# The embedding's products join the end of the recurrence's fill stream and wait in DRAM; ScalarE writes a pair's first right-hand side

## The chip, the cores and the metric

The kernel runs on one core of one Trainium2 chip. The metric is the device time of one launch in microseconds (us); the median of three runs is compared. The engines are named as in the profile: PE is TensorE (PEld its weight loads), DVE is VectorE, ACT is ScalarE, POOL is GpSimd, SP is SyncE, which here only issues transfers. ACTq and SPq are the sequencers of ACT and SP at work on the issue of a DMA.

## The reference, cut to what matters

One decoder layer over 512 tokens of width 2048, all in fp32:

```
z = rms_norm(x) @ w_in                  # r, k, v, lora inputs, gates, pool input
y_rwkv = delta-rule recurrence over r, w, k, v, kk, a (16 heads of 64), group norm, bonus, gate
y_pool = causal window means, a small linear map per group, gate
x = x + concat(y_rwkv, y_pool) @ w_out
gate = sigmoid(x @ w_pg + b_pg)
x = x + gate * (p @ w_ple)              # p: 512 x 256, w_ple: 256 x 2048
out = rms_norm(x)
```

The embedding term p @ w_ple depends on nothing that the kernel computes: both factors are inputs.

## The kernel before, in words

Every large product is made of three fp32r products (high by high, high by low, low by high) of operands that are split into a rounded part and a rest: `split` and `wsplit` cast on ACT and subtract on DVE. One such product of 128 by 128 weights with 512 columns is called a product below.

**Recurrence.** The 16 heads are worked through as 8 pairs j, each in 8 chunks ch of 64 tokens (`recur`). A chunk is a chain of small steps: py on PE (`py <- sbd, ar`), the right-hand side zs on DVE (`zs <- py, mv`, L721), pu on PE, two copies to uv on ACT (L731), ps on PE, the new state sbd on DVE (L742; L740 in the first chunk), and again py. In the first chunk there is no py: zs is a plain copy of mv on DVE (L725), where mv is what ACT copied out of the accumulator pmv (L648) in `gather`, before `recur` starts. While such a step runs on DVE or ACT, PE works on a stream of unrelated products (`stream`): the projections z of later pairs and the 16 units of the pool group (`pool_unit`, tile names zb and pp). `pump(n)` takes about n products from the stream, in units of 3, and carries what it overdrew to the next call. HC is the fill of the three legs of a chunk (py to pu, pu to ps, ps to py), H1 to H5 and HX are that of places in `gather` and between the pairs. All of PE's instructions of this part keep the order in which they are written. DVE and ACT take the work in an order that the scheduler fixes when the program is compiled.

**Between the parts.** After the last pair the stream is pumped by H2, `finish` turns the last pair's output on PE (pyt), scales it (yo) and writes it to the DRAM tensor yd (`yd <- yo`). The pools of the recurrence are then closed (`rw`, about a hundred kilobytes of each partition, among them) and the rest of the stream is drained. Then p is turned on PE (ppt) and split into phi and plo. At the start of the kernel the pool `xp` is closed in the same way ahead of `rw`; its last use is the turning of the parameters on PE (pt_prm, L296). The pool units of the stream use no tile of `rw`. The pool `ymp`, which takes the memory that `rw` left, gets the 16 rows of yd back (yin, three buffers) and their split halves yhi and ylo.

**Projections.** w_out and then w_pg are streamed in 4 column blocks ec of 512 (`proj`, accumulators acc_o and acc_g, 16 steps k by 4 token tiles tt by 3 products each). After a block of w_out the new x is added on DVE, written to x2d, and turned on PE (px) for the second projection. `embed(ec)` makes one block of p @ w_ple: 24 products, 4 copies to SBUF on ACT (L923). `embed(0)` stands behind the last block of w_out, `embed(ec + 1)` behind block ec of w_pg, ahead of that block's `gate`. In this part PE's order is the scheduler's. Accumulators rotate over five banks.

Of the kernel before, what the change touches and what calls it, by code (L numbers as in the profile page):

```python
# [34 lines left out]
def trunk_kernel(ctx: ExitStack, tc: tile.TileContext, x, p, norm_g, w_in, mu, w0, w_up, a0, a_up,  # L35
# [123 lines left out]
    def tr(*a):  # L159
        i = nc.tensor.transpose(*a)  # L160
        return tc.keep_in_program_order(i) if pin[0] else i

    def mm3(ps, wh, wl, xh, xl, first, last):
        mm(ps, wh, xh, start=first, stop=False)
        mm(ps, wh, xl, start=False, stop=False)
        mm(ps, wl, xh, start=False, stop=last)


    plan, ready = [], {}
# [23 lines left out]
    for j in range(NJ):  # L193
        if j + 1 < NJ:
            jobs += [("z", nm, j + 1) for nm in "krv"]
        jobs += [("b", None, n_ + i) for i in range(nfill[j])]
        n_ += nfill[j]
        if j + 1 < NJ:
            jobs += [("z", "g", j + 1)]
    plan_cols(O_L, "l")  # L200
    for kind, nm, j in jobs:
        if kind == "z":
            plan_cols({"r": O_R, "k": O_K, "v": O_V, "g": O_G}[nm] + j * P, f"{nm}{j}")
        else:
            g, i = j // 4, j % 2
            if j % 4 < 2:
                plan_cols(O_U + g * 256 + i * P, f"b{j}")
            else:
                plan_cols(O_GP + g * 256 + i * P, f"b{j}")
                plan.append((f"wp{j}", 0, w_pool[0, g, :, i * P:(i + 1) * P].rearrange("(k p) n -> p k n", p=P), 2, P))  # L210
# [174 lines left out]
    def pool_unit(n):  # L385
# [31 lines left out]
        nc.vector.scalar_tensor_tensor(sgp, pq, dp(73, m), sgp, ALU.mult, ALU.mult)  # L417
        nc.scalar.dma_start(out=yd[NJ + m], in_=sgp)

    def stream():  # L420
        for kind, nm, j in jobs:
            if kind == "b":
                yield from pool_unit(j)
                continue
            ps = psA.tile([P, T], F32, name=f"z{nm}{j}", tag="acc")
            yield from zcols(ps, f"{nm}{j}")
            t_ = rw.tile([P, T], F32, name=f"s{nm}{j}", tag=f"s{nm}", bufs=2)
            if nm == "g":
                silu2(ps, t_)
            else:  # L430
                shifted(ps, t_, {"r": 0, "k": 8, "v": 16}[nm] + j)
            zt[nm, j] = t_
# [18 lines left out]

    pws, kks, late = {}, {}, [None]

    H1, H2, H3, H4, H5 = 6, 16, 20, 6, 10

    def decay_and_rate(j):

# [156 lines left out]
    def gather(j):  # L614
# [26 lines left out]
        for u in range(8):  # L641
            for par in range(2):
# [2 lines left out]
                mm(ps[pb:pb + 64, u, :], mt[kb:kb + 64, par, u, 1 - par, :],  # L645
                   uv[kb:kb + 64, 2 * (u // 2) + par, 64 * h:64 * h + 64], start=True, stop=True)
        mv = rw.tile([P, 4, P], F32, name=f"mv{j}", tag="mv")
        nc.scalar.copy(mv.rearrange("p q (h t) -> p (q h) t", h=2), ps)  # L648

        d.update(uv=uv, bkn=bkn, mv=mv)  # L650
# [40 lines left out]
    def recur(j, work, between):  # L691
# [17 lines left out]
        for ch in range(NCH):  # L709
# [8 lines left out]
            if ch > 0:  # L718
                mm(py[:, sl], ar[:, q, 2 * par:2 * par + 2, :], cur, start=ch in (1, 4), stop=True,
                                 skip_group_check=True)  # L720
                lead[0] = nc.vector.tensor_tensor(zs[pb:pb + 64], py[pb:pb + 64, sl], mv[pb:pb + 64, q, :], ALU.add)  # L721
                step()
                pump(HC1)
            else:
                nc.vector.tensor_copy(zs[pb:pb + 64], mv[pb:pb + 64, q, :])  # L725

            psu = psS.tile([P, T], F32, name=f"pu{j}_{ch}", tag="s")
            mm(psu[:, 0:P], x1[:, 2 * q:2 * q + 2, :], zs, start=True, stop=True)
# [71 lines left out]

        pending.append(finish)

    HC, HT, HX = (7, 7, 8), 130, 24
    HS, HN = 9, 3
    pending = []
    need("k", 0)
# [13 lines left out]
    for j in range(NJ):  # L820
        def between():
            pump(H3)
            if j + 1 < NJ:
                scores(j + 1)
                pump(H2)

        if j + 1 < NJ:
            prepare(j + 1)
        recur(j, invert(j + 1) if j + 1 < NJ else iter(()), between)
        if j + 1 < NJ:  # L830
            gather(j + 1)
    pump(H2)
    pending.pop()()
    s2a.close()
    psB = ctx.enter_context(tc.tile_pool(name="psB", bufs=3, space=PSUM))
    lp = ctx.enter_context(tc.tile_pool(name="lp", bufs=1))
    pn = []
    for h in range(2):
        t_ = lp.tile([P, 2, DPLE], F32, name=f"pn{h}", tag="ple", bufs=4)
        nc.scalar.dma_start(out=t_, in_=p[256 * h:256 * h + 256, :].rearrange("(t p) q -> p t q", p=P))  # L840
        pn.append(t_)
    phi = lp.tile([P, 2, T], F32R, name="phi", bufs=1)
    plo = lp.tile([P, 2, T], F32R, name="plo", bufs=1)
    pump(10 ** 6)
    pin[0] = False
    for k in range(2):
        pt = psM.tile([P, T], F32, name=f"ppt{k}", tag="m")
        for tt in range(NT):
            nc.tensor.transpose(pt[:, tt * P:(tt + 1) * P], pn[tt // 2][:, tt % 2, k * P:(k + 1) * P], ident)
        split(phi[:, k, :], plo[:, k, :], pt)  # L850
    sy = ctx.enter_context(ExitStack())
    ymp = sy.enter_context(tc.tile_pool(name="ymp", bufs=1))
    yhi = ymp.tile([P, KT, T], F32R, name="yhi")
# [11 lines left out]
    EC = 512  # L865
    KEEP = 8
    TP = 40
    AS = (3,)
# [8 lines left out]
    def proj(w, hi_, lo_, ec, nm, ks=range(KT), tts=range(NT), keep=None):  # L877
        acc = {tt: acc_tile(f"acc_{nm}{ec}_{tt}") for tt in tts}
        if keep is not None:
            acc = {tt: [acc[tt]] if tt < NT - 1 else [acc[tt][:, 0:EC // 2], acc_tile("acc_h")[:, 0:EC // 2]]  # L880
                   for tt in tts}
        for i, k in enumerate(ks):
            src = w[k * P:(k + 1) * P, ec * EC:(ec + 1) * EC].unsqueeze(1)
            if keep is None or i < KT - KEEP:
                wh, wl = wsplit(src, 1, EC, f"{nm}{ec}_{k}")
            else:
                raw = wp.tile([P, 1, EC], F32, name=f"raw_{nm}{ec}_{k}", tag="raw")
                nc.sync.dma_start(out=raw, in_=src)
                own = i < KT - 4
                wh = (kp_ if own else wp).tile([P, 1, EC], F32R, name=f"whk{k}", tag=f"whk{k}" if own else "whi")  # L890
                wl = (kp_ if own else wp).tile([P, 1, EC], F32R, name=f"wlk{k}", tag=f"wlk{k}" if own else "wlo")
                split(wh, wl, raw)
                keep[k] = (wh, wl)
                continue
            for tt in tts:
                ts_ = slice(tt * P, (tt + 1) * P)
                parts = acc[tt] if keep is not None else [acc[tt]]
                hw = EC // len(parts)
                for h, a_ in enumerate(parts):
                    hc = slice(h * hw, h * hw + hw)  # L900
                    mm3(a_, hi_[:, k, ts_], lo_[:, k, ts_], wh[:, 0, hc], wl[:, 0, hc], i == 0, i == KT - 1)
        return acc

    ples = {}

    def embed(ec, pool):
        es = slice(ec * EC, (ec + 1) * EC)
        src = w_ple[:, es].rearrange("(k p) n -> p k n", p=P)
        ph, pl = [], []
        for k in range(2):  # L910
            a_, b_ = wsplit(src[:, k:k + 1, :], 1, EC, f"ple{ec}_{k}")
            ph.append(a_)
            pl.append(b_)
        ple = []
        for tt in range(NT):
            ts_ = slice(tt * P, (tt + 1) * P)
            pq = psM.tile([P, EC], F32, name=f"pple{ec}_{tt}", tag="m")
            for k in range(2):
                nc.tensor.matmul(pq, phi[:, k, ts_], ph[k][:, 0, :], start=k == 0, stop=False)  # L919
                nc.tensor.matmul(pq, phi[:, k, ts_], pl[k][:, 0, :], start=False, stop=False)  # L920
                nc.tensor.matmul(pq, plo[:, k, ts_], ph[k][:, 0, :], start=False, stop=k == 1)  # L921
            t_ = pool.tile([P, EC], F32, name=f"ple{ec}_{tt}", tag="ple", bufs=4)
            nc.scalar.copy(t_, pq)  # L923
            ple.append(t_)
        ples[ec] = ple

    for ec in range(D // EC):
        es = slice(ec * EC, (ec + 1) * EC)
        acc = proj(w_out, yhi, ylo, ec, "o", order)
        x2 = []  # L930
        for tt in range(NT):
            rows = slice(tt * P, (tt + 1) * P)
            t_ = pp.tile([P, EC], F32, name=f"x2_{ec}_{tt}", tag=("u", "sw")[tt // 2])
            nc.scalar.dma_start(out=t_, in_=x[rows, es])
            nc.vector.tensor_tensor(t_, acc[tt], t_, ALU.add)
            nc.scalar.dma_start(out=x2d[rows, es], in_=t_)
            x2.append(t_)
        if ec == D // EC - 1:
            embed(0, lp)
        for i in range(EC // P):  # L940
            pt = psM.tile([P, T], F32, name=f"px2_{ec}_{i}", tag="m")
            for tt in range(NT):
                nc.tensor.transpose(pt[:, tt * P:(tt + 1) * P], x2[tt][:, i * P:(i + 1) * P], ident)  # L943
            split(x2hi[:, 4 * ec + i, :], x2lo[:, 4 * ec + i, :], pt)

    sy.close()

# [1 line left out]
    with tc.tile_pool(name="fp", bufs=2) as fp, tc.tile_pool(name="kp_", bufs=1) as kp_:  # L949
# [65 lines left out]
        for ec in range(LAST):  # L1015
            ple = ples.pop(ec)
            pre = {}
            vec = vectors(ec)
            acc = proj(w_pg, x2hi, x2lo, ec, "g")
            embed(ec + 1, fp if ec % 2 == 0 else lp)  # L1020
            for tt in range(NT):
                fetch(ec, tt)
                gate(acc[tt], ec, tt, slice(ec * EC, (ec + 1) * EC), ec)
# [41 lines left out]
```

## Time and profile before

| | us |
|---|---|
| median of three runs | 1122.82 (1122.77 to 1124.36) |
| the profiled execution, its own time | 1124.35 |
| its span, first to last instruction | 1122.6 |
| PE busy | 1081.4 |
| DVE busy | 709.3 |
| ACT busy | 459.9 |

The profile is of one execution. Its span lacks the 1.75 us around the program that its own time has. A busy time is the union of an engine's instructions; matmuls are pipelined, so their busy time tells when PE had work, not how densely it was fed.

### The profile page before, as it was taken

What the parts mean: (1) busy time and instruction counts of PE and PEld (TensorE: products, weight loads), DVE (VectorE), ACT (ScalarE), POOL (GpSimd) and SP (SyncE); (2) the same over time, 40 slices, a digit from 0 to 9 for tenths busy, and PEclk for the clock granted to TensorE, in tenths of its full rate; (3) what the DMA queues carried; (4) which work ended last, traced back from release to release, by engine and by line L of the source; (5) the groups of instructions that cost most, each with busy time, mean ns of one, the idle gap of its engine ahead of it and who ended that gap; (6) DMA issues with size and microseconds to landing.
All of it is one profiled execution on the core that took longest, in us unless ns stands there. A gap on an engine that the chain in (4) does not pass through costs nothing. (4 is left out here: it accounts for less than half of the span.)

```text
span 1122.6 us, 17272 instructions
## 1 busy us (share of the span) xinstructions
PE 1081.4 (96%) x6090; PEld 880.6 (78%) x6090; DVE 709.3 (63%) x1861; ACT 459.9 (41%) x920; POOL 75.2 (7%) x184
## 2 busy tenths in 40 slices
PE   5999999999999998999999999999999999999995
PEld 4888887877877876878778787778888888888885
DVE  6677868778588687687885955564243332525446
ACT  7643536336336353363362343252222232424333
POOL 2100010110110100101101102000000000000001
PEclk9999999999999998999999999999999999999998
DMA  7433332423423332324234233465343444434244
GB/s 228 122 92 96 101 105 69 114 85 82 121 78 93 99 77 71 100 74 110 79 89 120 74 104 96 150 215 174 115 161 125 138 145 155 150 104 151 94 132 150
DMA packets 173877, 130.17 MB, mean 116 GB/s; under 512 B 34165, under 2 KB 139230, under 8 KB 173790
## 3 DMA queue, kind: packets, MB, share of 16 engines
q1 hardware_dynamic: 157694, 103.89, 31.6%
q10 hardware_dynamic: 16096, 25.17, 6.9%
q8 instruction: 48, 0.79, 0.3%
q14 instruction: 39, 0.32, 0.1%
HBM read 113.82 MB, written 14.68 MB: 114 GB/s over the span
## 5 line engine op out<-in xcount | busy, mean ns | idle before, releaser
L133 DVE TENSOR_TENSOR wlo_g<-raw_g,whi_g 128x512 fp32r<-128x512 f32 x88 | 59.4, 684 | 78.6 <-ACT whi_g L132 78.4
L156 PE MATMUL zb<-hhi,whi_b 128*128 128x512 f32 x256 | 107.2, 419 | 0.0
L133 DVE TENSOR_TENSOR wlo_o<-raw_o,whi_o 128x512 fp32r<-128x512 f32 x64 | 43.8, 691 | 93.7 <-ACT whi_o L132 93.7
L156 PE MATMUL acc_o<-wlo_o,yhi 128*128 128x512 f32 x256 | 99.9, 390 | 0.6 <-DVE wlo_o L133 0.6
L156 PE MATMUL zb<-hhi,wlo_b 128*128 128x512 f32 x256 | 100.5, 392 | 0.0
L156 PE MATMUL acc_o<-whi_o,ylo 128*128 128x512 f32 x256 | 100.3, 392 | 0.0
L132 ACT CAST whi_g<-raw_g 128x512 fp32r<-128x512 f32 x88 | 54.3, 623 | 112.2 <-PE acc_g L156 62.1
L156 PE MATMUL zb<-hlo,whi_b 128*128 128x512 f32 x256 | 100.0, 391 | 0.0
L156 PE MATMUL acc_o<-whi_o,yhi 128*128 128x512 f32 x256 | 99.4, 391 | 0.5 <-ACT yhi L137 0.5
L156 PE MATMUL acc_g<-whi_g,x2hi 128*128 128x512 f32 x224 | 86.5, 386 | 0.0
L156 PE MATMUL acc_g<-wlo_g,x2hi 128*128 128x512 f32 x224 | 86.4, 386 | 0.0
L156 PE MATMUL acc_g<-whi_g,x2lo 128*128 128x512 f32 x224 | 86.3, 385 | 0.0
L132 ACT CAST whi_o<-raw_o 128x512 fp32r<-128x512 f32 x64 | 39.7, 623 | 101.1 <-PE acc_o L156 93.6
L749 POOL TENSOR_SCALAR s0p<-sbd,pw 64x64 f32<-64x64 f32 x96 | 52.9, 551 | 331.9 <-DVE sbd L742 255.3
L132 ACT CAST whi_b<-raw_b 128x512 fp32r<-128x512 f32 x64 | 39.6, 619 | 73.5 <-PE zv L156 27.7
L133 DVE TENSOR_TENSOR wlo_b<-raw_b,whi_b 128x512 fp32r<-128x512 f32 x64 | 43.8, 685 | 29.0 <-ACT whi_b L132 28.5
L156 PEld LDWEIGHTS acc_o<-wlo_o,yhi 128*128 128x128 f32 x256 | 48.1, 188 | 11.4 <-DVE wlo_o L133 1.5
L156 PEld LDWEIGHTS zb<-hhi,wlo_b 128*128 128x128 f32 x256 | 48.0, 188 | 10.9
L156 PEld LDWEIGHTS acc_o<-whi_o,yhi 128*128 128x128 f32 x256 | 48.1, 188 | 10.5 <-ACT yhi L137 0.7
L156 PEld LDWEIGHTS acc_o<-whi_o,ylo 128*128 128x128 f32 x256 | 48.1, 188 | 10.0 <-DVE ylo L138 0.4
L597 DVE TENSOR_TENSOR xw<-xw,tm 128x60 f32<-128x60 f32 (+24 forms) x248 | 51.9, 209 | 6.3
L156 PEld LDWEIGHTS zb<-hhi,whi_b 128*128 128x128 f32 x256 | 48.3, 189 | 8.7
(290 smaller groups left out, 2568.2 us busy)
## 6 DMA issues: line engine op xcount, KB each, us to landing
raw_b<-in_w_in_dram SPq DMA_DIRECT2D x64, 256.0 KB
raw_o<-in_w_out_dram SPq DMA_DIRECT2D x64, 256.0 KB
raw_g<-in_w_pg_dram SPq DMA_DIRECT2D x64, 256.0 KB
raw_k<-in_w_in_dram SPq DMA_DIRECT2D x32, 256.0 KB
raw_r<-in_w_in_dram SPq DMA_DIRECT2D x32, 256.0 KB
raw_v<-in_w_in_dram SPq DMA_DIRECT2D x32, 256.0 KB
raw_g<-in_w_in_dram SPq DMA_DIRECT2D x32, 256.0 KB
n<-nd SPq DMA_DIRECT2D x16, 256.0 KB
```

The lines of the kernel that those rows point to most:

```text
L132: nc.scalar.copy(hi, raw)
L133: nc.vector.tensor_tensor(lo, raw, hi.bitcast(F32), ALU.subtract)
L156: i = nc.tensor.matmul(*a, **k)
L597: nc.vector.tensor_tensor(xw[:, 0:n_, s + 1:32], xw[:, 0:n_, s + 1:32], tm[:, 0:n_, 0:w_], ALU.add)
L749: nc.gpsimd.tensor_scalar(s0p[hc, :], nxt[hc, hc], pcn[hc], None, ALU.mult)
```

## The change

The 4 blocks of the embedding become the last jobs of the stream (`embed_unit`). Their products accumulate in psA, ACT copies each 128 by 512 result to SBUF, into buffers that the pool group used, and writes it to a new DRAM tensor pled from its own queue. p is loaded at the start of the last pair and turned in that pair's first chunk, into tiles of the pool `rw` (tags ar and mt). `recall(ec)` reads the blocks back at the places where `embed` stood. The turning of the last block of x2 is handed to `proj` as `aside` and issued behind its third step k. The constants of the fill are set anew: HC (7, 7, 8) becomes (8, 8, 8), H3 20 becomes 16, H4 6 becomes 8, HX 24 becomes 16, and the fill ahead of the last `finish` 16 becomes HE = 32. And in `gather` ACT writes the first chunk's zs straight out of the accumulator, where DVE copied it from mv in `recur`.

```diff
+    EC = 512
+    pled = dram.tile([T, D], F32, name="pled", bufs=1)
+    jobs += [("e", None, ec) for ec in range(D // EC)]
...
+        elif kind == "e":
+            for k in range(2):
+                plan.append((f"e{j}_{k}", 0, w_ple[k * P:(k + 1) * P, j * EC:(j + 1) * EC].unsqueeze(1), 1, EC))
...
+    def embed_unit(ec):
+        ws = [chunk(f"e{ec}_{k}", 0) for k in range(2)]
+        phi, plo = phl
+        for tt in range(NT):
+            ts_ = slice(tt * P, (tt + 1) * P)
+            pq = psA.tile([P, EC], F32, name=f"pple{ec}_{tt}", tag="acc")
+            for k in range(2):
+                wh, wl = ws[k]
+                mm(pq, phi[:, k, ts_], wh[:, 0, :], start=k == 0, stop=False)
+                mm(pq, phi[:, k, ts_], wl[:, 0, :], start=False, stop=False)
+                mm(pq, plo[:, k, ts_], wh[:, 0, :], start=False, stop=k == 1)
+                if k == 0:
+                    yield 3
+            t_ = pp.tile([P, EC], F32, name=f"ple{ec}_{tt}", tag=("u", "sw")[tt % 2])
+            nc.scalar.copy(t_, pq)
+            nc.scalar.dma_start(out=pled[ts_, ec * EC:(ec + 1) * EC], in_=t_)
+            yield 3
...
-    H1, H2, H3, H4, H5 = 6, 16, 20, 6, 10
+    H1, H2, H3, H4, H5, HE = 6, 16, 16, 8, 10, 32
...
         mv = rw.tile([P, 4, P], F32, name=f"mv{j}", tag="mv")
+        nc.scalar.copy(zsp[0][64:128, :].rearrange("p (h t) -> p h t", h=2), ps[64:128, 0:2, :])
         nc.scalar.copy(mv.rearrange("p q (h t) -> p (q h) t", h=2), ps)
...
-            else:
-                nc.vector.tensor_copy(zs[pb:pb + 64], mv[pb:pb + 64, q, :])
...
-    HC, HT, HX = (7, 7, 8), 130, 24
+    HC, HT, HX = (8, 8, 8), 130, 16
...
+                phl.extend((hl[:, 0], hl[:, 1]))
+                for k in range(2):
+                    pt = psM.tile([P, T], F32, name=f"ppt{k}", tag="m")
+                    for tt in range(NT):
+                        tr(pt[:, tt * P:(tt + 1) * P], pn[:, tt, k * P:(k + 1) * P], ident)
+                    split(phl[0][:, k, :], phl[1][:, k, :], pt)
...
+        if j + 1 == NJ:
+            pn = rw.tile([P, NT, DPLE], F32, name="pn", tag="ar", bufs=2)
+            for h in range(2):
+                nc.scalar.dma_start(out=pn[:, 2 * h:2 * h + 2, :],
+                                    in_=p[256 * h:256 * h + 256, :].rearrange("(t p) q -> p t q", p=P))
+            hl = rw.tile([P, 2, 2, T], F32R, name="hl", tag="mt", bufs=2)
...
-    pump(H2)
+    pump(HE)
     pending.pop()()
     s2a.close()
     psB = ctx.enter_context(tc.tile_pool(name="psB", bufs=3, space=PSUM))
     lp = ctx.enter_context(tc.tile_pool(name="lp", bufs=1))
-    pn = []
-    for h in range(2):
-        t_ = lp.tile([P, 2, DPLE], F32, name=f"pn{h}", tag="ple", bufs=4)
-        nc.scalar.dma_start(out=t_, in_=p[256 * h:256 * h + 256, :].rearrange("(t p) q -> p t q", p=P))
-        pn.append(t_)
-    phi = lp.tile([P, 2, T], F32R, name="phi", bufs=1)
-    plo = lp.tile([P, 2, T], F32R, name="plo", bufs=1)
     pump(10 ** 6)
     pin[0] = False
...
+            if aside is not None and i == 2:
+                with tc.issue_after(e_.ins):
+                    aside()
         return acc
...
-    def embed(ec, pool):
...
+    def recall(ec, pool):
+        ples[ec] = []
...
+            t_ = pool.tile([P, EC], F32, name=f"pler{ec}_{tt}", tag="ple", bufs=4)
+            nc.scalar.dma_start(out=t_, in_=pled[tt * P:(tt + 1) * P, ec * EC:(ec + 1) * EC])
+            ples[ec].append(t_)
...
-            embed(0, lp)
+            recall(0, lp)
...
+        if ec < D // EC - 1:
+            turn()
...
-            acc = proj(w_pg, x2hi, x2lo, ec, "g")
-            embed(ec + 1, fp if ec % 2 == 0 else lp)
+            acc = proj(w_pg, x2hi, x2lo, ec, "g", aside=turn if ec == 0 else None)
+            recall(ec + 1, fp if ec % 2 == 0 else lp)
```

## Rows read from the trace of the kernel before

**Rows 1.** Windows: length, busy PE, PEld, DVE, ACT, POOL; PEclk, DMA share, GB/s

```profile
145.00:645.00 500.00, 485.77 (x3074) 389.15 (x3073) 384.14 (x1178) 217.85 (x455) 52.91 (x100) 0.99 0.33 91
731.00:1094.00 363.00, 362.43 (x1648) 299.71 (x1647) 151.50 (x234) 122.15 (x220) 0.00 (x0) 1.00 0.44 143
```

**Rows 2.** Waits of PE from 56 to 756: us in total, times, longest

```profile
PE py L156 <- DVE sbd L742: 4.2, 7, 1.5
PE pu L156 <- issue: 3.3, 1, 3.3
PE pu L156 <- DVE zs L721: 2.6, 5, 0.6
PE ps L156 <- ACT uv L731: 2.3, 3, 1.2
PE pyt L160 <- DVE ysb L787: 1.6, 3, 1.1
```

**Rows 3.** Timeline at the first chunk of a pair: start, duration, what, [idle before]

```profile
434.87 0.22 DVE L725 COPY zs<-mv 64x128 f32<-64x128 f32 x1
...
435.19 0.76 PE L156 MATMUL pu<-zs,x 128*128 128x128 f32 x2 [3.31 <-issue]
...
436.18 0.63 PE L156 MATMUL zg<-hlo,whi_g 128*128 128x512 f32 x1
```

**Rows 4.** Windows behind that wait, columns as in Rows 1

```profile
435.00:440.00 5.00, 4.81 (x13) 3.99 (x14) 2.46 (x6) 1.65 (x4) 0.65 (x1) 0.50 0.01 3
440.00:445.00 5.00, 5.00 (x21) 3.99 (x19) 0.87 (x2) 0.62 (x1) 0.61 (x2) 0.88 0.18 52
```

**Rows 5.** Timeline of PE, the step py with and without a wait

```profile
674.28 0.49 PE L156 MATMUL py<-sbd,ar 128*128 128x128 f32 x2 [0.37 <-DVE sbd L742]
674.52 0.48 PE L156 MATMUL zb<-hhi,whi_b 128*128 128x512 f32 x1
...
680.57 0.38 PE L156 MATMUL py<-sbd,ar 128*128 128x128 f32 x2
680.71 0.47 PE L156 MATMUL zb<-hhi,whi_b 128*128 128x512 f32 x1
```

**Rows 6.** Instructions by tile: count, ns min/median/max, first and last start

```profile
L923 ACT COPY ple<-pple x16: 567/588/590, 913.7 to 1066.7; 128x512 f32<-128x512 f32 x16
...
L648 ACT COPY mv<-pmv x8: 576/588/607, 117.0 to 649.2; 128x512 f32<-128x512 f32 x8
L725 DVE COPY zs<-mv x8: 175/224/225, 117.9 to 652.0; 64x128 f32<-64x128 f32 x8
```

**Rows 7.** Timeline of PE at the end of the recurrence

```profile
716.90 0.77 PE L160 MATMUL pyt<-ident,ysb 128*128 128x128 f32 x2 [1.10 <-DVE ysb L787]
...
729.29 0.87 PE L849 MATMUL ppt<-ident,pn 128*128 128x128 f32 x6 [0.25 <-DMA pn<-in_p_dram]
730.65 0.50 PE L156 MATMUL acc_o<-whi_o,yhi 128*128 128x512 f32 x1 [0.48 <-ACT yhi L137]
```

**Rows 8.** Chain that ended last, there: start, us, what

```profile
721.08 3.33 DMA yd<-yo
...
725.47 4.48 DMA yin<-yd
...
729.98 0.62 ACT yhi L137
```

**Rows 9.** Timeline of POOL, its first write into the recurrence's pool

```profile
36.11 0.20 POOL L346 MEMSET uaz<- 64x128 f32 x1 [28.54 <-PE pt_prm L296]
```

**Rows 10.** Chain that ended last, in the projections

```profile
777.46 0.33 PE px L943 x3
777.79 2.08 PE acc_o L156 x9
...
968.56 43.52 PE acc_g L156 x192
```

**Rows 11.** Timeline of DVE, the gates behind a block of w_pg

```profile
966.71 1.28 DVE L973 TENSOR_TENSOR gt<-acc_g,bB 128x512 f32<-128x512 f32 x2
```

More of the change, by code (lines that the diff above doesn't have):

```diff
@@ L165, in mm3 @@
         mm(ps, wh, xl, start=False, stop=False)
-        mm(ps, wl, xh, start=False, stop=last)
+        return mm(ps, wl, xh, start=False, stop=last)
     plan, ready = [], {}
@@ L418, in pool_unit @@
         nc.scalar.dma_start(out=yd[NJ + m], in_=sgp)
+    phl = []
+    def embed_unit(ec):
[15 more added lines that the diff above has]
+            yield 3
     def stream():
@@ L423, in stream @@
                 yield from pool_unit(j)
+                continue
+            if kind == "e":
+                yield from embed_unit(j)
                 continue
@@ L825, in between @@
                 pump(H2)
+            else:
+                phl.extend((hl[:, 0], hl[:, 1]))
[10 more added lines that the diff above has]
+            hl = rw.tile([P, 2, 2, T], F32R, name="hl", tag="mt", bufs=2)
         if j + 1 < NJ:
@@ L836, in trunk_kernel @@
     lp = ctx.enter_context(tc.tile_pool(name="lp", bufs=1))
-    pn = []
-    for h in range(2):
-        t_ = lp.tile([P, 2, DPLE], F32, name=f"pn{h}", tag="ple", bufs=4)
-        nc.scalar.dma_start(out=t_, in_=p[256 * h:256 * h + 256, :].rearrange("(t p) q -> p t q", p=P))
-        pn.append(t_)
-    phi = lp.tile([P, 2, T], F32R, name="phi", bufs=1)
-    plo = lp.tile([P, 2, T], F32R, name="plo", bufs=1)
     pump(10 ** 6)
     pin[0] = False
[L846 to L850, printed above, removed]
     sy = ctx.enter_context(ExitStack())
@@ L864, in trunk_kernel @@
     x2d = dram.tile([T, D], F32, name="x2d", bufs=1)
-    EC = 512
     KEEP = 8
@@ L875, in acc_tile, with proj @@
         return pool.tile([P, EC], F32, name=nm, tag=tag)
-    def proj(w, hi_, lo_, ec, nm, ks=range(KT), tts=range(NT), keep=None):
+    def proj(w, hi_, lo_, ec, nm, ks=range(KT), tts=range(NT), keep=None, aside=None):
         acc = {tt: acc_tile(f"acc_{nm}{ec}_{tt}") for tt in tts}
@@ L900, in proj @@
                     hc = slice(h * hw, h * hw + hw)
-                    mm3(a_, hi_[:, k, ts_], lo_[:, k, ts_], wh[:, 0, hc], wl[:, 0, hc], i == 0, i == KT - 1)
+                    e_ = mm3(a_, hi_[:, k, ts_], lo_[:, k, ts_], wh[:, 0, hc], wl[:, 0, hc], i == 0, i == KT - 1)
+            if aside is not None and i == 2:
+                with tc.issue_after(e_.ins):
+                    aside()
         return acc
     ples = {}
-    def embed(ec, pool):
[L907 to L914, printed above, removed]
-        for tt in range(NT):
[L916 to L925, printed above, removed]
+    def recall(ec, pool):
+        ples[ec] = []
+        for tt in range(NT):
+            t_ = pool.tile([P, EC], F32, name=f"pler{ec}_{tt}", tag="ple", bufs=4)
+            nc.scalar.dma_start(out=t_, in_=pled[tt * P:(tt + 1) * P, ec * EC:(ec + 1) * EC])
+            ples[ec].append(t_)
     for ec in range(D // EC):
@@ L938, in trunk_kernel, with turn @@
         if ec == D // EC - 1:
-            embed(0, lp)
[L940 to L944, printed above, removed]
+            recall(0, lp)
+        def turn(ec=ec, x2=x2):
+            for i in range(EC // P):
+                pt = psM.tile([P, T], F32, name=f"px2_{ec}_{i}", tag="m")
+                for tt in range(NT):
+                    nc.tensor.transpose(pt[:, tt * P:(tt + 1) * P], x2[tt][:, i * P:(i + 1) * P], ident)
+                split(x2hi[:, 4 * ec + i, :], x2lo[:, 4 * ec + i, :], pt)
+        if ec < D // EC - 1:
+            turn()
     sy.close()
```

## The prediction

> **What bounds the kernel now.** I read the windows of the two long parts first, then PE's waits, then the timeline around each, and last the chain through the seam between the parts. In the projections PE is busy for all but 0.6 of 363 us, in the recurrence for all but 14.2 of 500 [rows 1]. So PE is the bound everywhere, and moving 96 products from the projections into the stream saves nothing by itself: 192 products took 43.52 us [rows 10], 0.2267 each, and the 21.8 us of the embedding only change place. The change can win only PE time that now goes to waiting, and lose by making PE wait anew. The waits of the recurrence are listed in [rows 2]: three legs of the chunk chain (4.2, 2.6 and 2.3 us in 7, 5 and 3 waits), the turning of the output (1.6) and one single wait of 3.3 us.
>
> The Trainium skill (Perfetto Trace Analysis, Identifying the Most-Contended Engine) says that matmul busy time flatters PE and that the share of weight loads is the better measure. By that measure, 389 of 500 us against 300 of 363 [rows 1], the recurrence could be fed 6% denser, an estimate of 29 us where idle time shows 14; the small products of the chain explain a part of the difference, so the sum below goes by idle time.
>
> **The first right-hand side.** The single wait is put down to "issue", but the timeline shows its end: DVE's copy of mv to zs ran at 434.87 for 0.22, and PE's pu started 0.10 behind it [rows 3]. Its source mv is made in `gather`, before the pair's chunks begin, so the copy was late only by its place in DVE's fixed order. In the other seven pairs no wait for L725 appears in [rows 2]. What follows the wait is dearer than it looks: the granted clock is 0.50 in the next 5 us and 0.88 in the 5 after [rows 4], that is 1.2 GHz for a while. Lost: 5 x 0.50 + 5 x 0.12 = 3.1 us. With the zs written by ACT in `gather`, the wait goes, and with it the clock's fall: -3.3 - 3.1 = -6.4. DVE's next step towards PE, the first sbd, has the fill H3 and the scores between it and its reader, so I price what is late next at nothing; without that cover it would be the remainder of the same DVE queue, up to 1 us. ACT pays 8 copies, between 0.22 (the DVE copy of that size) and 0.59 (mv, four times the size) each [rows 6]; ACT is busy for 218 of 500 us [rows 1], which hides them. Behind the new copy stand mv and the key's square root, whose readers come much later. Bounds: -3.3 if the clock falls at another wait anyway, -6.4.
>
> **The fill.** I count the pump's units by its own rule. Of the 176 legs, 97 had a fill of 6 products and 79 of 9; now 59 and 117. By place, 64 legs rise from 6 to 9 and 26 fall. The 15 waits of [rows 2] on these legs are rows of the timeline like the first of [rows 5]; counting the products ahead of each, 14 are on legs of 6. Ten of them, 5.2 us together, lie on legs that rise, none longer than the 0.68 us that three products bring. That is the upper bound. The lower one takes averages: legs of 6 waited 7.5 / 97 = 0.077 each, those of 9 had one, the longest, 1.5 / 79 = 0.019, so the new mix would wait 59 x 0.077 + 117 x 0.019 = 6.8 instead of 9.0, a gain of 2.2. I take 4.5, nearer to the count by place, less what falling legs lose. Each wait also delays what stands behind it: from py to the next product 0.24 with a wait and 0.14 without [rows 5]; ten times 0.1 is 1.0. Together -5.5 (-2.2 to -6.2). The last `finish` stands behind 39 products instead of 24, 3.4 us more, and its first wait of 1.10 [rows 7] goes: -1.1.
>
> The places that pay are H3 and HX, 12 products a pair, against 2 more at H4. No wait for their operands shows in [rows 2], so there is some margin; I take +0.5, between 0 and seven waits like the 0.37 of [rows 5], 2.6.
>
> **The drain.** By the same count only 6 of the 96 embedding products stand ahead of the last `finish`; 90 products, 20.4 us, follow it, where 45 did. Each of the 16 results costs ACT a copy of 0.59 [rows 6] and a DMA issue, and takes one of two accumulators, against 1.36 us of PE per result. ACT has 8 casts of weights beside it. I take +0.5, between 0 and 16 x 0.15 = 2.4 if ACT paces it. The turning of p (8 small matmuls) only changes place.
>
> **The seam.** This is the largest loss that I see. The first reload, yin, started at 725.47, about 1 us after yd <- yo (721.08 + 3.33) had landed, and took 4.48; the cast to yhi took 0.62 and PE went on at 730.65 [rows 7, 8]. Most rows of yd had been written hundreds of us before. What held them is the memory: at the start of the kernel POOL's memset of a tile that needs no data waited 28.54 us, until the last reader of the closed pool xp was through [rows 9]. So a new pool waits for the whole of the pool whose room it takes. Now hl, the split p, lies in `rw` and is read until the last product of the drain. Then yin starts only there: PE stands for 4.48 + 0.62 + about 0.1 = 5.2 us, longer than the 3.3 that brought the clock down, so I add the 3.1 again. Against it the present waits of 0.25 and 0.48 [rows 7] go: +7.6. Bounds: -0.7, if the reload isn't held by hl, and +8.3.
>
> **The projections.** Without `embed`, block ec + 1 of w_pg follows block ec at once. The second pair of gates frees its accumulators at 966.71 + 1.28 [rows 11], while the products of the next block started at 968.56 [rows 10], behind 24 embedding products of 5.4 us. Starting those 5.4 us earlier, the one that needs the third gate's bank would wait 2.3, three times 6.9. But at the edges of w_out PE's order has later products between the turnings px that wait [rows 10]; the scheduler fills such holes. I take +0.5 (0 to 6.9). The last px behind step k = 2 of the next projection has 36 products, 8.2 us, to cover it, more than the 5.4 of now. `recall` loads lie a whole block ahead of use.
>
> **Sum.** -6.4 - 5.5 - 1.1 + 0.5 + 0.5 + 7.6 + 0.5 = -3.9 us. The profiled execution's own 1124.35 becomes 1120.5; it lies 1.5 above the median of the runs, so against 1122.82 I forecast 1118.9. Its own range is 1115 to 1123.
>
> **Rivals.**
> - *The reload is not held.* If the wait counts only what `rw` had to do before it was closed, or only the bytes that overlap, the loads run under the 20 us drain. Then the seam gives -0.7 instead of +7.6: -12.2, 1110.6. For it: the drain is long enough (the chain from yo to yhi needs 9.5 us [rows 8]). Against it: [rows 9]. Chance 0.25.
> - *The written blocks pace the drain* (slower). A result buffer is free when its DMA has landed; four buffers go round in 5.4 us of PE. With a copy of 0.59 and an issue, a landing may take 4.5 us; yd <- yo took 3.33 and yin 4.48 [rows 8], with weights for w_ple and w_out coming in beside them. If a landing takes 6.5, a round takes 7.5, and 15 results lose 0.5 each, +7.6: 1126.5. It decides from landings of about 6 us. Chance 0.12. The Trainium skill (DMA: Bandwidth & Descriptors, Issuing engines are not separate DMA queues) says that transfers issued by different engines share the same 16 DMA engines. By that rule ACT's queue for pled gives no shelter from SP's weights; no row here shows a drain with both.
> - *The fill gains nothing*: the new waits at H3, HX and the falling legs eat the raised ones. Then -3.9 + 5.5 = +1.6, 1124.4. For it: DVE is busy for 384 of 500 us [rows 1], and a wait caused by a full DVE queue moves with it. Against it: 14 of 15 waits on legs of 6. Chance 0.13.
>
> The forecast keeps 0.5. Leaving out a tenth at either end, the range is 1109.5 to 1124.5. About 0.2%, 2.2 us, is what a measurement of this kernel can tell. Faster by more: the first rival, and two thirds to four fifths of the forecast, 0.63. Same: 0.2, the rest of the forecast and half of the third rival. Slower: 0.17.
>
> **What would show it.** Right: no wait at the first pu of any pair and a clock of 1.00 there; waits on the three legs down from 9.0 to about 4.5 us; a hole in PE of about 5 us between the last pple and the first acc_o, yin's first load starting inside it, and a lower clock behind it. If yin starts during the drain, the first rival holds. Results of pple further apart than 1.4 us in the drain show the second. A wait of acc_g at the block edges would show that I was wrong there. The prediction fails most easily at the seam, where one choice of two is worth 8 us.

## The result, and the profile after

| | before | after |
|---|---|---|
| median of the runs, us | 1122.8 (1120.8 to 1124.4, 4 runs) | 1127.8 (1126.0 to 1128.2, 4 runs) |
| the profiled execution, its own time and span | 1124.35, 1122.6 | 1126.0, 1124.3 |

The kernel became slower: the ratio is 1.0044, with a 95% interval of 1.0031 to 1.0056, or about 5 us. The forecast was 1118.9, in a range of 1109.5 to 1124.5. The two profiled executions are only 1.7 us apart, since that of before was the slowest of its four and that of after the fastest. The mean granted clock was 0.994 in the profiled run of after and 0.991 to 0.992 in its other three. So the profile of after shows the waits well, but perhaps not all that the clock costs; an experiment with the same recurrence (e4) shows below what may be missing.

Windows of the two long parts, as in [rows 1]:

```profile
145.00:645.00 500.00, 489.19 (x3110) 394.20 (x3109) 386.23 (x1185) 222.47 (x465) 48.16 (x98) 1.00 0.34 93
753.00:1094.00 341.00, 341.00 (x1545) 282.30 (x1545) 143.25 (x221) 108.46 (x192) 0.00 (x0) 0.99 0.49 159
```

In the projections PE has no gap at all, so the edges of the blocks cost nothing. The recurrence has 10.8 us without PE instead of 14.2: 3.4 less, which is the one wait of [rows 3] and no more. Waits of PE from 56 to 756, as in [rows 2]:

```profile
PE acc_o L156 <- ACT yhi L137: 6.3, 1, 6.3
PE py L156 <- DVE sbd L772: 5.2, 8, 1.1
PE pq L156 <- DVE y L701: 3.1, 2, 1.9
PE pu L156 <- DVE zs L753: 1.0, 2, 0.7
PE pple L156 <- ACT ple L444: 0.9, 1, 0.9
PE pp L156 <- ACT uv L658: 0.9, 1, 0.9
PE pu L156 <- ACT x L719: 0.9, 1, 0.9
PE pmv L156 <- ACT bkn L667: 0.9, 1, 0.9
PE pss L156 <- ACT bkn L667: 0.8, 1, 0.8
PE pm L156 <- DVE bk L572: 0.3, 1, 0.3
PE ps L156 <- ACT uv L761: 0.3, 1, 0.3
```

Three things stand here. The wait of 3.3 us at a first pu is gone, and so is the 1.6 of pyt. The three legs wait 6.5 us (py 5.2, pu for zs 1.0, ps 0.3) instead of 9.1. And there is a group that the kernel before hardly had, at the turn from one pair to the next: pq, pp, pu behind x, pmv, pss, pm. Here pbk, pmv, pss, pq and px are steps of `gather` on PE, in this order, pm is one of `scores`, pp a product of the pool group in the stream that waits here for ACT's copies of uv, and pu behind x a first pu that waits for what ACT makes of px. With px (0.2, not shown) the group is 7.1 us. Before, the same places had 2.2: pss 1.4, pbk 0.5 and 0.3 of a pyt other than the last `finish`'s. Of the 7.1 us only pq and pm, 3.4, stand right behind HX and H3, the fills that were shortened.

The seam came as forecast. PE's timeline there, answering [rows 7], and the chain through it, answering [rows 8]:

```profile
746.02 0.39 PE L156 MATMUL pple<-whi_e,hl 128*128 128x512 f32 x1
752.71 0.77 PE L156 MATMUL acc_o<-whi_o,yhi 128*128 128x512 f32 x1 [6.30 <-ACT yhi L137]
```

```profile
729.39 6.12 DMA pled<-ple
...
736.17 10.25 PE pple L156 x42
746.45 0.59 ACT ple L444
747.06 0.33 ACTq L445
747.39 0.04 issue
747.43 4.54 DMA yin<-yd
751.99 0.63 ACT yhi L137
```

The first yin starts 1.0 us behind the last product of the embedding, though yd had been written long before. The hole is 6.3 us where 5.2 was forecast, because ACT's copy of the last result (0.59) and the issue of its write (0.33) stand ahead of the load. The clock behind the hole, as in [rows 4]:

```profile
750.00:755.00 5.00, 2.29 (x6) 1.80 (x7) 2.49 (x5) 2.28 (x4) 0.00 (x0) 0.67 0.65 209
755.00:760.00 5.00, 5.00 (x16) 3.96 (x15) 1.83 (x3) 1.49 (x3) 0.00 (x0) 0.65 0.78 252
```

A mean of 0.67 and 0.65 is a mixture of the two levels, 1.2 and 2.4 GHz. The products behind the hole stand 0.43 us apart, against 0.23 elsewhere.

### The profile page after: what moved, and what is told of

It reads as the page before. It is cut to its first block, busy times and chain, and to the rows that moved or that the text cites. A ratio compares the mean times of both kernels' runs of the same rounds, so it can differ in the third digit from the quotient of the medians.

```text
span 1124.3 us, 17316 instructions
## 1 busy us (share of the span) xinstructions
PE 1080.0 (96%) x6090; PEld 881.1 (78%) x6090; DVE 708.0 (63%) x1853; ACT 465.5 (41%) x928; POOL 71.6 (6%) x184
## 5 line engine op out<-in xcount | busy, mean ns | idle before, releaser
L156 PE MATMUL acc_g<-whi_g,x2hi 128*128 128x512 f32 (+1 forms) x224 | 86.7, 387 | 0.0
L156 PE MATMUL acc_g<-wlo_g,x2hi 128*128 128x512 f32 (+1 forms) x224 | 86.4, 386 | 0.0
L779 POOL TENSOR_SCALAR s0p<-sbd,pw 64x64 f32<-64x64 f32 x96 | 49.5, 516 | 343.2 <-DVE sbd L772 261.2
```

The costliest lines, as they stand in the source:

```text
L156: i = nc.tensor.matmul(*a, **k)
L779: nc.gpsimd.tensor_scalar(s0p[hc, :], nxt[hc, hc], pcn[hc], None, ALU.mult)
```

## The experiments

**The parts by themselves: e1, e2, e3.** e1 is the kernel before with ScalarE's copy alone:

```diff
         mv = rw.tile([P, 4, P], F32, name=f"mv{j}", tag="mv")
+        nc.scalar.copy(zsp[0][64:128, :].rearrange("p (h t) -> p h t", h=2), ps[64:128, 0:2, :])
...
-            else:
-                nc.vector.tensor_copy(zs[pb:pb + 64], mv[pb:pb + 64, q, :])
```

> The kernel before, with only ScalarE's copy of the first chunk's zs (and without DVE's). Theory 1 (the single wait and the fall of the clock behind it go, nothing follows): 3.3 to 6.9 us faster than before, about 1116 to 1119.5, no first pu with a wait, granted clock 1.00 through the whole recurrence. Theory 2 (the wait moves on to the next step of the same DVE queue, or ACT's extra copy delays uv): within 1.5 us of before.

Measured: 1117.84 against 1122.33, ratio 0.9959 (0.9944 to 0.9974), 4.5 us faster. Windows of e1 at the place of [rows 4]:

```profile
430.00:435.00 5.00, 5.00 (x54) 4.22 (x53) 4.61 (x11) 2.74 (x7) 0.65 (x1) 1.00 0.60 184
435.00:440.00 5.00, 5.00 (x33) 3.98 (x33) 3.78 (x9) 1.14 (x2) 1.26 (x2) 1.00 0.32 92
```

No hole, and the clock stays at 1.00. Its profiled run is 6.4 us shorter than that of before, the sum of the prediction to the digit; that is in part chance, since the profiled run of before was the slowest of its four. By medians it is less, 4.5.

e2 is the kernel before with the new constants alone; e3 is the changed kernel with the old ones:

```diff
-    H1, H2, H3, H4, H5, HE = 6, 16, 16, 8, 10, 32
+    H1, H2, H3, H4, H5, HE = 6, 16, 20, 6, 10, 32
...
-    HC, HT, HX = (8, 8, 8), 130, 16
+    HC, HT, HX = (7, 7, 8), 130, 24
```

> The kernel before, with only the new constants of the fill (HC 8,8,8, H3 16, H4 8, HX 16). Theory 1 (as predicted, legs gain): 2 to 6 us faster. Theory 2 (what the trace after suggests: pu and ps wait 4.4 us less, py 1.2 more and the two turnings behind the shortened HX 3.8 more): within 1 us of before, and waits of PE on pq for DVE's y of 1 to 2 us each, of which the kernel before has none.

> The changed kernel with the fill constants of before (HC 7,7,8, H3 20, H4 6, HX 24; HE stays 32). If the new constants are worth 2 to 6 us, 2 to 6 us slower than the changed kernel, about 1130 to 1134. If they are worth nothing, the same 1126 to 1128. If they cost something at HX, up to 3 us faster than it.

e2 took 1138.1, ratio 1.0141 (1.0123 to 1.0158), far from what either theory gave. It is no clean measure: without the embedding the stream runs out earlier, and PE stood 8.5 us ahead of ppt, for the load of p, which begins only when the last `finish` is through. Besides, the first pu waited 5.1 us in two pairs. It does show the two waits on pq, 3.1 us together. e3 is clean: 1124.83, ratio 1.0021 (1.0013 to 1.0030), while the changed kernel stands at 1.0044 (1.0031 to 1.0056). So the new constants cost 2.6 us by the ratios and 3.0 by the medians, and the embedding, with its seam, drain and last `finish`, costs 7.0 (e3 against e1). e3's legs:

```profile
PE py L156 <- DVE sbd L772: 3.8, 6, 1.5
PE pu L156 <- DVE zs L753: 2.6, 5, 0.7
PE ps L156 <- ACT uv L761: 2.3, 3, 1.2
```

**What holds the reload: e4, e7, e8, e15.** e4 gives the split p a home outside `rw`, so that the pool's last reader is the last `finish`:

```diff
+    mp = ctx.enter_context(tc.tile_pool(name="mp", bufs=1))
     s2a = ctx.enter_context(ExitStack())
...
-        mt = rw.tile([P, 2, 8, 2, C], F32, name=f"mt{j}", tag="mt", bufs=2)
+        mt = (rw if j % 2 else mp).tile([P, 2, 8, 2, C], F32, name=f"mt{j}", tag="mt")
...
-            hl = rw.tile([P, 2, 2, T], F32R, name="hl", tag="mt", bufs=2)
+            hl = mp.tile([P, 2, 2, T], F32R, name="hl", tag="mt")
```

> The changed kernel, with the split p in a pool of its own that stays open, so that the recurrence's pool has its last reader in the last finish and not in the last product of the embedding. Theory 1 (the closed pool held the reload): yin starts under the drain, the 6.46 us between the last pple and the first acc_o go, and the lower clock behind them: 8 to 10 us faster than the changed kernel, about 1118. Theory 2 (the reload waits for something else in ACT's queue, such as the writes of pled): no gain, 1126 to 1128.

Measured: 1128.1, ratio 1.0053 (1.0039 to 1.0067), no gain, as theory 2 had it. Timeline of ACT in e4's drain:

```profile
733.46 0.33 ACTq L891 DMA_DIRECT2D yin<-yd  x1
...
742.79 0.58 ACT L445 COPY ple<-pple 128x512 f32<-128x512 f32 x1 [1.85 <-DMA pled<-ple]
...
743.84 0.39 ACTq L891 DMA_DIRECT2D yin<-yd  x1
...
749.20 0.33 ACTq L891 DMA_DIRECT2D yin<-yd  x1
...
752.64 0.61 ACT L132 CAST whi_o<-raw_o 128x512 fp32r<-128x512 f32 x1
```

The pool did hold the load: with hl elsewhere the first yin starts at 733.46, 15 us ahead of the last pple, where it had started behind it. But the next ones stand in ACT's queue between the copies of the embedding, which wait for writes to land, and the first casts of w_out, two of which stood at 739.98 and 744.13 in the changed kernel, come at 752.64, behind casts yhi that wait for their loads. One wait was taken away and two took its place: PE's waits on pple and acc_o are 8.2 us together, against 7.2 in the changed kernel. e4 also has the recurrence of the changed kernel, and shows what the profile of that one lacks, a fall of the clock behind the second wait on pq:

```profile
505.00:510.00 5.00, 3.16 (x44) 1.95 (x44) 4.94 (x6) 1.78 (x4) 0.00 (x0) 0.87 0.34 105
510.00:515.00 5.00, 5.00 (x49) 4.23 (x50) 3.53 (x6) 1.81 (x6) 0.70 (x1) 0.79 0.19 52
```

In 5 x 0.13 + 5 x 0.21 this is up to 1.7 us, of the size that separates the other three runs of the changed kernel from its profiled one (1.6 to 2.2). None of the three was profiled, so that this is the reason is argued, not shown.

e7 has the old fill, hl outside, and the loads issued by GpSimd; e8 also puts half of the embedding's results into four more buffers:

```diff
-        nc.scalar.dma_start(out=t_, in_=yd[k])
+        nc.gpsimd.dma_start(out=t_, in_=yd[k])
...
-            t_ = pp.tile([P, EC], F32, name=f"ple{ec}_{tt}", tag=("u", "sw")[tt % 2])
+            pl_, tg_ = (pp, ("u", "sw")[tt % 2]) if not lpo or tt < 2 else (lpo[0], "ple")
+            t_ = pl_.tile([P, EC], F32, name=f"ple{ec}_{tt}", tag=tg_, bufs=4 if tg_ == "ple" else 2)
...
```

> The kernel of e3 (changed, old fill) with the split p outside the recurrence's pool as in e4, and the reloads yin issued from GpSimd's queue, where nothing stands ahead of them. Theory 1 (after the memory is free, ACT's queue is the second thing that holds the reload): the first loads land in the drain and the hole of 4.4 to 6.9 us ahead of the first acc_o goes below 2 us, 6 to 9 us faster than e3: 1116 to 1119. Theory 2 (the DMA engines are full of w_out and pled, so the loads land late from any queue): hole of 3 to 5 us, 1122 to 1125.

> As e7, with half of the embedding's results in four more buffers, so that none waits for its write to land. Theory 1 (the 6 us landings of pled pace ACT in the drain through the four buffers): the waits inside the drain (2.0 us in e3) go and ACT reaches w_out's casts earlier, 1 to 3 us faster than e7. Theory 2 (no pacing that matters): the same as e7 within 1 us.

Measured: e7 1123.44 (ratio 0.9998 to 1.0016), e8 1121.63 (0.9983 to 1.0001). So e7 gains 1.4 on e3, far less than theory 1 asked; its time lies where theory 2 had it. That theory's reason, loads that land late from any queue, is not what held the seam, for e15 below frees it with the loads on the same queue. The buffers gain 1.8 more, as expected of pacing by landings: the waits of pple fall from 3.4 to 1.7 us. What was left shows on ACT in e8:

```profile
746.97 0.62 ACT L137 CAST yhi<-yin 128x512 fp32r<-128x512 f32 x1 [0.21 <-DMA yin<-yd]
747.50 2.18 ACT L132 CAST whi_o<-raw_o 128x512 fp32r<-128x512 f32 x4
```

The first of these four casts is what the first acc_o needs, and PE stood for 3.1 us ahead of it: ACT's fixed order has it behind eight casts of yd. e14 is e8 with the one transpose of e11 (below), and e15 is e14 with the loads and casts of yd written step by step between the casts of w_out's first block:

```diff
-    for k in order:
-        t_ = ymp.tile([P, T], F32, name=f"yin{k}", tag="yin", bufs=3)
-        nc.gpsimd.dma_start(out=t_, in_=yd[k])
-        split(yhi[:, k, :], ylo[:, k, :], t_)
+    for _ in range(2):
+        load_y()
...
         for i, k in enumerate(ks):
+            load_y()
```

Here `load_y` does the body of the old loop for the next k.

> The kernel of e8 (repaired seam, old fill) with the one transpose. No wait on pq before, so 0 to 1 us faster than e8: about 1121.

> The kernel of e14, with the loads and casts of yd written between the casts of w_out's first block, so that whi_o no longer stands behind eight casts yhi in ACT's order. Theory 1 (that order is the third thing that holds the seam, and moving the embedding is worth nothing by itself once nothing holds it): the hole of 3.2 us ahead of the first acc_o goes below 1 us, 2 to 3 us faster than e14, 1119 to 1120, which is still no faster than e1 (1117.84). Theory 2 (the reloads themselves are late beside the writes of pled): the hole stays at 2 to 4 us or moves behind the first steps k, 1121 to 1123.

Measured: e14 1121.89, the same as e8; e15 1117.60, ratio 0.9963 (0.9950 to 0.9977), 4.3 us faster than e14 and more than theory 1 asked. Waits of PE in e15 behind the recurrence:

```profile
PE pple L156 <- ACT ple L446: 1.4, 2, 1.2
PE acc_o L156 <- ACT whi_o L132: 0.6, 1, 0.6
PE acc_o L156 <- DVE wlo_o L133: 0.3, 1, 0.3
```

Of the hole of the seam 0.9 us are left, in two waits. From e3 to e15 (the one transpose in it is worth nothing, by e14 and e8) the seam and the drain gave back 7.2 us, and where they are free the moved embedding is worth what the prediction said of it by itself, nothing: 1117.60 against e1's 1117.84.

**What the fill gains and where it pays: e5, e6.** e5 is the changed kernel with HX back at 24; e6 the changed kernel with all old constants but HC = (8, 8, 8).

> The changed kernel with HX alone set back from 16 to 24. Theory 1 (the shortened HX uncovers DVE's transpose y ahead of pq, and the 2.0 us wait at 504 brings the clock down in most executions): the two waits on pq go, 3 to 6 us faster than the changed kernel, 1122 to 1125. Theory 2 (the queue of DVE is late as a whole and the wait moves to the next reader): within 1 us of the changed kernel.

> The changed kernel with all constants of before but HC = 8,8,8: the legs rise, no place pays, only the drain is shorter. Against e3 (HC 7,7,8, 1124.8). Theory 1 (as predicted, legs of 9 hardly wait): waits on py, pu and ps down from 11.4 us to 4 to 7, so 4 to 7 us faster, 1118 to 1121. Theory 2 (the waits follow DVE's queue and not the fill of a leg): about the same waits, 1124 to 1126.

Measured: e5 1127.51 (ratio 1.0044), e6 1128.50 (1.0055). In e5 the waits on pq are gone, as theory 1 had it, but the time is the same, as theory 2 had it: pyt waits 3.5 us, px 0.9, pbk 0.9, pss 0.8. The longest wait of pyt is 2.3 us, at 434, for DVE's scalings of the pair's output (ysb); DVE was busy for all of the 5 us around it, and in the 5 us behind it the granted clock was 0.50. e6 is slower than either theory gave. In e6, to 800:

```profile
PE acc_o L156 <- DMA x<-in_x_dram: 10.0, 1, 10.0
PE pu L156 <- DVE zs L753: 2.3, 5, 0.7
PE pmv L156 <- ACT bkn L667: 1.9, 1, 1.9
PE py L156 <- DVE sbd L772: 1.7, 4, 0.6
PE pyt L160 <- DVE ysb L817: 1.7, 3, 0.9
PE pu L156 <- ACT x L719: 1.6, 2, 0.8
PE pss L156 <- ACT bkn L667: 1.0, 4, 0.3
PE ps L156 <- ACT uv L761: 0.2, 1, 0.2
```

The legs (py, pu behind zs, ps) wait 4.2 us against 8.7 in e3: raising them does what the prediction said. But the turn (pmv, pyt, pu behind x, pss) waits 6.2 against 2.2, although no place there is shorter than before. The waits of PE in the recurrence, in us:

| | HC | H3, H4, HX | legs | turn | sum |
|---|---|---|---|---|---|
| e3 | 7, 7, 8 | 20, 6, 24 | 8.7 | 2.2 | 10.9 |
| e6 | 8, 8, 8 | 20, 6, 24 | 4.2 | 6.2 | 10.4 |
| e5 | 8, 8, 8 | 16, 8, 24 | 4.7 | 6.3 | 11.0 |
| the changed kernel | 8, 8, 8 | 16, 8, 16 | 6.5 | 7.1 | 13.6 |

So the turn pays as soon as the legs are raised, whether its own places are shortened or not; the short HX decides where it pays (on pq instead of pyt) and adds to the sum. Why raised legs make the turn wait stays open. A constant also shifts which job of the stream, with its own steps for DVE and ACT, falls at which turn; that this is the reason is argued, not shown. Since e6's sum is no larger than that of e3, its loss of 3.7 us against e3 lies elsewhere. The granted clock fell to 0.75 and 0.90 from 350 to 360, behind the wait of 1.9 us on pmv. And at the seam the legs have used up the stream: the last `finish` ends 1.3 us ahead of the last pple, and PE stood 10.0 us ahead of acc_o, against 6.7. The trace puts that wait down to a load of x, but yin was on its way as well: its first load was issued at 751.45, behind the write of the last yo at 747.50.

**Why the turn pays: e9, e10, e11, e12.** PE's second wait on pq in the changed kernel, and DVE there:

```profile
506.25 0.69 PE L156 MATMUL pq<-y,mt 32*32 32x32 f32 x32 [1.86 <-DVE y L701]
```

```profile
504.64 0.42 DVE L701 STREAM_TRANSPOSE y<-x 32x256 f32<-32x256 f32 x1
505.00 0.64 DVE L408 SCALAR_TENSOR_TENSOR u<-sw,u 128x512 f32<-128x512 f32 x1
505.67 0.44 DVE L701 STREAM_TRANSPOSE y<-x 32x256 f32<-32x256 f32 x1
```

No line of DVE here has an idle time before it, and DVE was busy for 4.96 of the 5 us from 500 on: it works through its fixed order without a gap, and y comes when its turn comes. Here a shorter HX only lets PE arrive earlier: by 8 products, 1.8 us, and the wait is 1.86. It is the longer of the two waits on pq; at the other turns pq does not wait. If DVE is what is full, work taken from it should help. e9 (on the changed kernel) and e10 (on e1) give ACT the eight scalings of a pair's output, with one small DVE step more for the bias nm8:

```diff
...
         for i in range(8):
-            nc.vector.tensor_scalar(y8[:, i, :], y8[:, i, :], mvr[:, i, 0:1], rs8[:, i, :],
-                                    ALU.subtract, ALU.mult)
+            nc.scalar.activation(y8[:, i, :], y8[:, i, :], AF.Identity, scale=rs8[:, i, :], bias=nm8[:, i, :])
```

> The changed kernel, with the 8 scalings of a pair's output (y8, 1.87 us of DVE in a pair) done on ACT, with one small DVE step more for the bias. Theory 1 (at the turn of a pair DVE works without a gap, and what it makes for pq, pyt and pmv is late by the length of its queue, so a shorter HX and H3 only let PE arrive earlier): the two waits on pq fall from 3.1 to under 1.0 us in total and the clock no longer falls there; 2 to 6 us faster than the changed kernel. Theory 2 (what is late is the way of x1 through DRAM, or ACT): waits at the turn as they are or longer, 0 to 3 us slower.

> The kernel of e1 (before, with ScalarE's zs) with the same 8 scalings on ACT. Theory 1: the waits of the turns and the wait of py for sbd of 1.7 us in pair 6 shrink, 1 to 4 us faster than e1, 1114 to 1117. Theory 2: ACT, which makes uv and the casts of the weights, is late in its turn: the same as e1 within 1 us, or slower.

Measured: e9 1144.1, ratio to before 1.0211 (1.0182 to 1.0239), e10 1137.5, 1.0127 (1.0108 to 1.0145): 16 us slower than the changed kernel and 20 us slower than e1. ACT and DVE in e10:

```profile
191.72 2.44 ACT L788 ACTIVATE ysb<-ysb,nm,rs 128x64 f32<-128x64 f32 x7
```

```profile
198.31 0.43 DVE L505 TENSOR_SCALAR kk<-kk 128x512 f32<-128x512 f32 x1 [2.91 <-ACT kk L504]
```

My theory fell in that form. ACT has no gap at that place either: the scalings took it 2.44 us for seven, and all behind them (bkn, zs, mv, kk) was late. ACT's kk starts at 197.68, where e1 has it at 194.09, and DVE in its turn stood 2.91 us for it. So e9 and e10 show that ACT is the wrong place for the work; that DVE would be faster with less of it they do not show.

e11 leaves the work where it is and takes away only the place in the order: both transposes y become one, on the changed kernel; e12 is e1 with the same edit.

```diff
-            for pb in (0, 64):
-                yt = nc.vector.transpose(y1[pb:pb + 32], x1[pb:pb + 32, :, 0:32])
+            yt = nc.vector.transpose(y1, x1[:, :, 0:32])
```

> The changed kernel, with DVE's two transposes y of 32 rows made as one of 128 rows, so that pq finds all of y at the place of the first. Theory 1 (the second y is late only by its place in DVE's fixed order, behind five steps of other work): the two waits on pq (3.1 us) go to under 0.5 and the clock no longer falls there, 2 to 5 us faster than the changed kernel, 1123 to 1126. Theory 2 (the turn as a whole is full, the next reader waits instead): within 1 us of the changed kernel, 1127 to 1128.5, with the same sum of waits.

> The kernel of e1 (before, with ScalarE's zs) with the one transpose y of e11. It has no wait on pq, so theory 1 gives 0 to 1 us from 8 transposes of 0.43 us that DVE is spared: 1116.8 to 1118. Theory 2 (any change of DVE's order moves waits at random): outside 1116 to 1119.

Measured: e11 1124.30, ratio 1.0020 (1.0011 to 1.0029), 3.5 us faster than the changed kernel, more than the 2.3 us by which the waits on pq fall (from 3.1 to 0.8), and its clock is at 1.00 through the recurrence. What is left of the wait:

```profile
PE pq L156 <- DVE y L700: 0.8, 1, 0.8
```

By the two profiled runs e11 is faster by 1.5 us only; that of the changed kernel lacks the fall of the clock. e12 took 1119.49 (0.9960 to 0.9982); that is outside 1116 to 1119, as theory 2 had it, but its interval overlaps that of e1, and the two are not told apart. So of the loss at the turn, this one step, with what followed from it, was 3.5 us by medians. With it gone the new constants are worth nothing: e11 1124.30, e3 1124.83.

**The fill with all else repaired: e13, e16.** e13 is e14, and e16 is e15, each with the new constants.

> The kernel of e8 (repaired seam) with the new fill constants and the one transpose. Against e14, which differs in the constants alone. Theory 1 (what cost the gain of the legs at the turn was the second y): 2 to 4 us faster than e14. Theory 2 (the other places at the turn, pmv, pp, pss and pm, pay as much as the legs gain): within 1 us of e14, or slower.

> The kernel of e15 (seam free, one transpose, old fill) with the new fill constants. In e13 a wait in the drain stood in the way of this comparison. Theory 1 (freed of the seam and of the second y, the raised legs gain what the prediction's lower end says): 1 to 3 us faster than e15, 1114.5 to 1116.5. Theory 2 (what the legs gain the other places at the turn pay, 11.2 against 11.7 us of waits in e13 and e14): within 1 us of e15, 1116.6 to 1118.6.

Measured: e13 1126.82 against e14's 1121.89, slower, as its theory 2 allowed; e16 1121.96, ratio 0.9997 (0.9988 to 1.0006), against e15's 1117.60. In the recurrence the sums of waits agree in both pairs (e16 11.3, e15 11.8), yet the new fill is 4.4 us slower in e16, outside what either theory gave. The place is the end of the recurrence. PE's turning of the pairs' outputs (count, ns min, median and max, first and last start), in e15 and then in e16:

```profile
L160 PE MATMUL pyt<-ident,ysb x32: 270/272/329, 193.4 to 714.8; 128*128 128x128 f32 x32
```

```profile
L160 PE MATMUL pyt<-ident,ysb x32: 270/272/329, 193.8 to 721.5; 128*128 128x128 f32 x32
```

The last one is 6.7 us later. What the legs take more of the stream is missing behind the last `finish`, where it covers the way of yd: in e15 30 products of the pool group and all 96 of the embedding stand behind it, in e16 90 of the embedding. So yd is written later and yin lands later, and ACT's order does the rest. In e16:

```profile
733.98 0.62 ACT L137 CAST yhi<-yin 128x512 fp32r<-128x512 f32 x1 [2.51 <-DMA yin<-yd]
...
734.50 1.07 ACT L446 COPY ple<-pple 128x512 f32<-128x512 f32 x2
```

The cast of the first yin stands in ACT's order ahead of copies that empty PE's accumulators. In e15 it waits 1.29 us, in e16 2.51 and in e13 5.10, and pple waits 1.4, 3.3 and 6.4 us in all. acc_o waits 2.4 in e16 instead of 0.9, and the granted clock falls to 0.84 and 0.82 from 725 to 735. With hl in `rw` none of this shows, since yin starts behind the last pple anyway: acc_o waits 6.7 us in e3 and 6.6 in e11.

## Why the prediction was wrong, point by point

**The first right-hand side**: right in its place, cause and clock. -6.4 in the profiled runs, -4.5 by the medians of e1, within the bounds of 3.3 to 6.4.

**The fill**: this step failed. Forecast -5.5, with +0.5 for the places that pay; measured +2.6 to +3.0, a miss of about 8 us, where the whole forecast missed by 8.9. Its first half held in part: the legs' waits fell by 2.6 in the changed kernel and by 4.5 with HC alone (e6), inside the bounds of 2.2 to 6.2; but the sign that was named for it, 4.5 us left on the legs, was missed with 6.5. What failed is the price of the turn, put at +0.5 and at most 2.6. It was 4.9 us of waits (7.1 against 2.2) and, where it shows, a fall of the clock behind the longest of them. "No wait for their operands shows, so there is some margin" took the absence of a wait for a margin. The upper bound, seven waits like 0.37, came from a leg, where PE waits for one short step; at pq and pyt it waits for a DVE that works without a gap. And the price was tied to the places that got shorter, H3 and HX. e6 and e5 show that this was too narrow: the turn waits 6.2 us with the legs raised and nothing shortened, and the sum of the recurrence's waits is 10.4 to 11.0 in e3, e5 and e6 alike. The legs' gain was moved, not won. What the legs took from the end of the stream had no price at all; it costs nothing while hl holds the seam (e11 against e3), and 4.4 us where the seam is free (e16 against e15). The third rival, that new waits eat the gain, was the right one in kind, with a chance of 0.13. It was priced at no gain (1124.4) and not as a loss, since it left the clock out. e11, without the second y, is the case that it describes, with no gain against e3; that its 1124.30 meets the rival's number is chance, since the other terms missed too.

**The last finish**: right. The 1.3 us of waits ahead of it are gone.

**The drain**: forecast +0.5, up to 2.4. pple waited 0.9 us in the changed kernel and 1.6 in e3. The second rival's mechanism is real (a landing took 6.12 us, its point of decision was about 6), but it struck one round, not 15. More buffers were worth 1.8 us (e8 against e7). The Trainium skill (DMA: Bandwidth & Descriptors, Issuing engines are not separate DMA queues) says that transfers interleave on the same 16 engines whoever issues them. The runs agree: loads of yd that GpSimd issued took 3.1 to 5.6 us on the chain of e7, those that ACT issued 3.1 to 4.4 us on that of e4. What e7 won, it did not win by faster loads.

**The seam**: right in place and size, and incomplete in cause. Seam and drain were forecast at 8.1 and are worth 7.2 (e3 to e15, with the old fill). The pool was the first thing that held the reload, as [rows 9] led to expect, but ACT's order, the buffers and the place of w_out's first cast stood right behind it; with the pool alone repaired (e4) the loss stayed. The first rival's 1110.6 did not come with a free pool.

**The projections**: no wait at the block edges, so 0 instead of +0.5.

Put together, the sizes are -4.5 for the right-hand side, +7.0 for the embedding with its seam, drain and finish (forecast -1.1 + 0.5 + 7.6 + 0.5 = 7.5), and +2.6 to +3.0 for the fill: +5.1 to +5.5, where 5.0 was measured. That this adds up is no test of the account, since e1 and e3 are steps on one way from the kernel before to the changed one. The part of the change that pays is its smallest one. e1 alone is 4.5 us faster than the kernel before; e15, which keeps the embedding in the stream, is no faster than that.

What stays open: why raised legs make the turn wait, and how often the clock falls behind the second wait on pq. Of the three profiles with the new fill and the same two waits on pq, those of e2 and e4 show it and that of the changed kernel doesn't.

## What to carry to other kernels

That no wait shows at a place doesn't say how much earlier its reader may come: look at the producer's engine there, and if its timeline has no idle time, take the reader's whole advance as the upper bound of the wait (here 1.86 us for 1.8 at one turn, less or nothing at the others). Filling one kind of wait can move it to another place, so compare the sum over the whole stretch. A stream of filler is one account: what is spent in one place is missing in another, and the last of it covers the turn to the next stage. And where several things hold a transfer (memory, its place in a queue, buffers, the order of its readers), taking away the first shows nothing until the last is gone.

## What the hardware showed that was not expected

- DVE's transpose of 128 by 256 in blocks of 32 took 0.44 us and one of 32 by 256 took 0.43 (medians), so one instruction in place of two saves a whole one. That it works in blocks of 32 by 32 is in the Trainium skill (VectorE: DVE Perf Modes, The three transpose paths); the equal time is from e11 and the changed kernel.
- The same scaling of 128 by 64 took DVE 1.88 us for eight in a row (changed kernel) and ACT 2.44 us for seven (e10), 0.24 and 0.35 each.
- GpSimd issued a load of 256 KB in 0.54 us (e7), ACT in 0.33 (changed kernel).
